# A two-layer encoder on one core: each step's rounded weights begin at an offset in their buffers

## The chip, the cores and the metric

The kernel runs on one core of one Trainium2 chip. The metric is the time of one execution on the device in microseconds. Before the change the median of two runs is 2566.06 us (2565.14 to 2566.98).

## What is computed

Two layers act on 256 tokens of width 2048. Each layer has three blocks, each with a residual sum: a mixer (projections `w_in` to three recurrences, then `w_out`), a cross attention to 256 memory rows, and a gated feed-forward block of width 5632. In short:

```python
for l in range(DEPTH):
    x = x + hybrid_mixer(rmsnorm(x, norm_mix[l]), ..., w_in[l], w_out[l], ...)
    x = x + memory_cross_attention(rmsnorm(x, norm_xattn[l]), rmsnorm(mem, norm_mem[l]), xa_wq[l], xa_wkv[l], xa_wo[l])
    x = x + conv_glu_ffn(rmsnorm(x, norm_ffn[l]), ffn_w_up[l], ffn_conv_w[l], ffn_conv_b[l], ffn_w_down[l])
return rmsnorm(x, norm_final)
```

All data are float32. Nearly all the work is `h @ w` with some 115 million weights in all, each of them read once from memory outside the core.

## The kernel before

The weights are cut into steps, in the order in which they are used (`layer_plan`, lines 64 to 119). A step holds seven or eight tiles of 128 x 128 weights (1024 or 896 columns in a buffer; two kinds are wider or take four row blocks at once). There are 890 steps. Each step's weights come by one DMA from the SyncE queue into a `raw` buffer (five of them).

A product of two float32 numbers is made of products of rounded ones (type float32r, which TensorE multiplies in one pass). So each weight is split into a rounded part `wh` and a rest `wl`: `split_w_hi` (line 1323) has ScalarE (ACT) copy `raw` to `wh` with rounding, and `split_w_lo` (line 1331) has VectorE (DVE) subtract `wh` from `raw` into `wl`. There are five `wh` and four `wl` buffers of WMAX = 1088 columns, that is 4352 bytes in each partition. The activations are split in the same way into a tile of 512 columns, rounded parts of 256 tokens and then the rests (`H`, and in later blocks `mo`, `mh`, `oT` and `g`).

The main loop (line 1450) goes through the steps: it issues the ACT split for the step three ahead, the DVE split for the step two ahead, and then this step's matmuls (`matmuls`, line 1345). A step of kind A takes each tile of weights as the stationary operand: with `form` 0, line 1360 multiplies the 512 moving columns with `wh`, and line 1361 the 256 rounded ones with `wl`. With `form` 1 (`xa_wo`, and the last tiles of all) there are three matmuls of 256 columns, lines 1363 to 1365. A step of kind B takes the activations as the stationary operand and the weights as the moving one, in slices of 256 or 264 columns (lines 1381 to 1383; 48 steps, 384 times three matmuls). Each matmul has a load of its stationary operand, which the profile shows apart as PEld.

Where things lie, in bytes in each partition: every `wh` and `wl` buffer begins at a place that is 64 modulo 256; a tile within it is 512 bytes further. `H`, and the pages that hold `mo`, `mh`, `oT` and `g`, begin at 224 modulo 256. Slices of 264 columns in kind B are 1056 bytes apart. Of the four slices of `UPAD` on which the convolutions work, two begin at an odd multiple of 16 bytes and two at a multiple of 32; the residual tiles `X` begin at a multiple of 32.

Between the steps' matmuls the loop runs the other work (norms, recurrences, attention, convolutions) as coroutines on ACT and DVE, with plain fp32 matmuls on TensorE. How many of them go ahead at each step is set by estimates of ACT's and DVE's time, which depend on the widths of the operands (`Metered`, lines 248 to 268).

Of the kernel before, what the change touches and what calls it, by code (L numbers as in the profile page):

```python
# [5 lines left out]
F32R = mybir.dt.float32r  # L6
# [5 lines left out]
P = 128  # L12
# [109 lines left out]
def step_len(st):  # L122
    if st["kind"] == "A":
        return P * len(st["tiles"])
    if st["kind"] == "B":
        return st["width"] * len(st["kts"])
    raise ValueError(st["kind"])
# [143 lines left out]
def build(tc, ws, xT, memT, par, con, masks, rot, dec, outT):  # L271
# [4 lines left out]
    pw = tc.alloc_tile_pool(name="weights", bufs=1)  # L276
# [39 lines left out]
    def nm(s):  # L316
        names[s] = names.get(s, 0) + 1
        return f"{s}_{names[s]}"
# [71 lines left out]
    def fn(out, src, f, **kw):  # L390

        want = "natural_log_exp_and_others" if f in (AF.Exp, AF.Ln) else "silu_and_others" if f in (AF.Silu, AF.Tanh) else table[0]
        if want != table[0]:
            act.preload_act_table_set(want)
            table[0] = want
        act.activation(out, src, f, **kw)

    def tt(out, a, b, op):
        dve.tensor_tensor(out, a, b, op)
# [900 lines left out]
    for l in range(NL):  # L1300
        gl, _ = group_steps(layer_plan(l))
        for off, g in gl:
# [3 lines left out]
            for st in g:  # L1306
                st = dict(st, l=l, g=gi, c=c, n=step_len(st))
# [4 lines left out]
    def load(gi):  # L1312
        if gi >= len(groups) or gi in raws:
            return
        l, off, g = groups[gi]
        t = pw.tile([P, GROUP_MAX], F32, name=nm("raw"), tag="raw", bufs=5)
        raws[gi] = t
        n = sum(step_len(st) for st in g)
        nc.sync.dma_start(t[:, :n], ws[l][off:off + P * n].rearrange("(p n) -> p n", p=P))

    WMAX = 1088

    def split_w_hi(j):
        if j < len(steps):
            st = steps[j]
            n = st["n"]
            st["raw"] = raws[st["g"]][:, st["c"]:st["c"] + n]
            st["wh"] = pw.tile([P, WMAX], F32R, name=nm("wh"), tag="wh", bufs=5)
            fn(st["wh"][:, :n], st["raw"], AF.Copy)

    def split_w_lo(j):
        if j < len(steps):
            st = steps[j]
            n = st["n"]
            st["wl"] = pw.tile([P, WMAX], F32R, name=nm("wl"), tag="wl", bufs=4)
            tt(st["wl"][:, :n], st["raw"], st["wh"][:, :n].bitcast(F32), ALU.subtract)
            if j + 1 == len(steps) or steps[j + 1]["g"] != st["g"]:
                load(st["g"] + 5)
            if j < 4:
                nc.sync.dma_start(X[2 + j // 2][:, j % 2 * 2:j % 2 * 2 + 2, :], xT[:, 8 + 2 * j:10 + 2 * j, :])  # L1340
# [46 lines left out]
    with tc.manual_schedule():  # L1387
# [57 lines left out]
        for j in range(2):  # L1445
            first_h(j)
            split_w_hi(j)
            split_w_lo(j)
        split_w_hi(2)
        for j, st in enumerate(steps):  # L1450
            if j == 0 or st["l"] != steps[j - 1]["l"]:
                for k, f in layer(st["l"]).items():
                    begins[(st["l"], k)] = f
            if 2 <= j + 2 < SINGLE + (KD - SINGLE) // 2:
                first_h(j + 2)
            split_w_hi(j + 3)
            split_w_lo(j + 2)
            for ev, ps in done:
                start(ev(ps), True)
            done.clear()  # L1460
            matmuls(st)
            if j == 5:
                fn(ONES, one, AF.Copy)
                nc.sync.dma_start(CON, con)
            if j == 7:
                nc.sync.dma_start(PAR[:, 0:PLAYER - KD], par[:, KD + T:PLAYER + T])
            if j == 11:
                nc.sync.dma_start(PAR[:, PLAYER - KD:], par[:, PLAYER + T:])
                mf = page(16, [P, 7, 64], F32, "mf")
                nc.sync.dma_start(mf, masks)  # L1470
                gp.tensor_copy(MSK, mf)
            if j == 15:
                start(gen_lb())
            advance(False)
            step_done(st["n"] / P * 0.325)
# [39 lines left out]
```

## Time and profile before

| | |
|---|---|
| median of two runs | 2566.06 us |
| the profiled execution | 2565.18 us, of which the span is 2563.3 us |
| TensorE busy | 2538.1 us (99%) |
| VectorE busy | 1925.6 us (75%) |
| ScalarE busy | 1469.8 us (57%) |
| mean granted share of TensorE's clock | 0.997 |

The span goes from the first to the last instruction. Matmuls overlap each other, so the pace of TensorE is read from the starts of matmuls, not from their durations.

### The profile page before, as it was taken

Reading aid. Unit: us, or ns where it says so; the run is one execution under the profiler, and the core shown is the slowest. Engines: PE = TensorE matmul, PEld = TensorE weight load, DVE = VectorE, ACT = ScalarE, POOL = GpSimd, SP = SyncE. Lnnn points to the kernel's source line nnn. Section 1 sums busy time; section 2 is a strip of 40 time slices with the busy share of each in tenths; the row PEclk is TensorE's granted clock in tenths of the full one; section 3 lists DMA queues with packets and bytes.
Section 4 is the critical chain, followed back from the end, with each engine's and each line's share of the span. In section 5 each row is a group of like instructions: output and inputs, shape, how many; then the busy total and the mean of one; then the engine's idle time right before and its main releaser. Section 6 shows DMA issues by size and latency. Waiting matters only on the chain.

```text
span 2563.3 us, 40208 instructions
## 1 busy us (share of the span) xinstructions
PE 2538.1 (99%) x15456; PEld 2252.9 (88%) x15456; DVE 1925.6 (75%) x3028; ACT 1469.8 (57%) x2152; POOL 4.9 (0%) x12
## 2 busy tenths in 40 slices
PE   9999989999999999999999999999999999999998
PEld 8888978998888888888898888889988888888887
DVE  7998788768776567776678888876877765677765
ACT  6866566566554345555466756655665543555543
POOL 0000000000000000000000000000000000000000
PEclk9999999999999999999999999999999999999999
DMA  7556656556665666665665575675566666666664
GB/s 272 170 170 205 194 161 197 186 172 190 190 190 183 193 195 192 190 189 186 191 192 163 154 236 181 189 217 170 175 196 189 189 187 191 194 188 193 189 183 131
DMA packets 141104, 482.02 MB, mean 188 GB/s; under 512 B 15280, under 2 KB 21360, under 8 KB 140912
## 3 DMA queue, kind: packets, MB, share of 16 engines
q1 hardware_dynamic: 140624, 479.17, 60.4%
q8 instruction: 122, 2.00, 0.3%
q14 instruction: 70, 0.57, 0.1%
q10 hardware_dynamic: 288, 0.27, 0.0%
HBM read 477.25 MB, written 2.13 MB: 187 GB/s over the span
## 4 chain that ended last, share of the span: by engine, by line
PE 97%; DVE 2%; DMA 0%; ACT 0%; issue 0%; DVEq 0%; SPq 0%; ACTq 0%
PE pj L1360 57%; PE pj L1361 29%; PE pj L1381 2%; PE pj L1382 2%; PE pj L1383 2%; PE pj L1364 1%; PE pj L1363 1%; PE pj L1365 1%; DVE wl L267 1%; PE ms L798 0%; PE ms L700 0%; PE ms L964 0%; DVE w L267 0%; DVE xbc L267 0%; PE ms L1152 0%; PE ms L1186 0%
## 5 line engine op out<-in xcount | busy, mean ns | idle before, releaser
L1360 PE MATMUL pj<-H,wh 128*128 128x512 f32 x4480 | 1561.0, 393 | 0.5 <-DVE H L267 0.5
L267 DVE TENSOR_TENSOR wl<-raw,wh 128x1024 fp32r<-128x1024 f32 (+2 forms) x894 | 1076.4, 1206 | 418.3 <-PE pj L1361 220.8
L267 ACT ACTIVATE wh<-raw 128x1024 fp32r<-128x1024 f32 (+2 forms) x894 | 933.4, 1048 | 658.2 <-PE pj L1360 351.8
L1361 PE MATMUL pj<-H,wl 128*128 128x256 f32 x4480 | 1253.1, 280 | 4.1 <-DVE wl L267 4.1
L1360 PEld LDWEIGHTS pj<-H,wh 128*128 128x128 f32 x4480 | 841.4, 188 | 186.5 <-ACT wh L267 1.1
L1361 PEld LDWEIGHTS pj<-H,wl 128*128 128x128 f32 x4480 | 841.5, 188 | 6.4 <-DVE wl L267 5.8
L1360 PE MATMUL pj<-g,wh 128*128 128x512 f32 x1386 | 480.7, 392 | 0.0
L1361 PE MATMUL pj<-g,wl 128*128 128x256 f32 x1386 | 387.4, 280 | 0.0
L1360 PEld LDWEIGHTS pj<-g,wh 128*128 128x128 f32 x1386 | 260.2, 188 | 57.4
L1361 PEld LDWEIGHTS pj<-g,wl 128*128 128x128 f32 x1386 | 260.2, 188 | 0.0
L267 ACT COPY e<-pj 128x256 f32<-128x256 f32 x288 | 106.4, 370 | 240.9 <-PE pj L1361 236.1
L1360 PE MATMUL pj<-mo,wh 128*128 128x512 f32 x512 | 179.7, 395 | 7.2 <-DVE mo L267 7.2
L267 DVE SCALAR_TENSOR_TENSOR ya<-UPAD,PAR,ya 128x256 f32<-128x256 f32 x352 | 146.5, 478 | 0.0
L1361 PE MATMUL pj<-mo,wl 128*128 128x256 f32 x512 | 143.9, 281 | 0.0
L267 DVE TENSOR_TENSOR X<-X,pj 128x256 f32<-128x256 f32 x167 | 70.0, 420 | 83.3 <-PE pj L1361 73.7
L1360 PEld LDWEIGHTS pj<-mo,wh 128*128 128x128 f32 x512 | 97.1, 190 | 29.2 <-DVE mo L267 7.6
L1361 PEld LDWEIGHTS pj<-mo,wl 128*128 128x128 f32 x512 | 97.1, 190 | 0.0
L267 ACT ACTIVATE ya<-UPAD,PAR 128x256 f32<-128x256 f32 x176 | 94.9, 588 | 1.2 <-DVE g L267 1.2
L267 DVE TENSOR_TENSOR UPAD<-pj,e 128x256 f32<-128x256 f32 x208 | 86.4, 418 | 0.2
L267 DVE TENSOR_TENSOR UPAD<-UPAD,R 128x512 f32<-128x512 f32 (+1 forms) x120 | 74.3, 621 | 4.0
L1381 PE MATMUL pj<-wh,H 128*128 128x264 f32 (+1 forms) x256 | 73.1, 285 | 0.0
L1383 PE MATMUL pj<-wh,H 128*128 128x264 f32 (+1 forms) x256 | 72.6, 284 | 0.0
(283 smaller groups left out, 1956.4 us busy)
## 6 DMA issues: line engine op xcount, KB each, us to landing
raw<-ws SPq DMA_DIRECT2D x778, 512.0 KB, 4.1
raw<-ws SPq DMA_DIRECT2D x96, 448.0 KB, 3.4
raw<-ws SPq DMA_DIRECT2D x16, 528.0 KB, 3.9
DE<-CD SPq DMA_DIRECT2D x8, 512.0 KB, 4.6
ya<-memT SPq DMA_DIRECT2D x16, 256.0 KB, 4.9
DS<-CD SPq DMA_DIRECT2D x8, 256.0 KB, 5.9
X<-xT SPq DMA_DIRECT2D x6, 256.0 KB, 7.2
outT<-y SPq DMA_DIRECT2D x3, 512.0 KB, 2.9
```

Of the source, the lines that this page charges most:

```text
L267: return f(out, *a, **k)
L1360: pe.matmul(ps, wh[:, a], s, start=first, stop=False)
L1361: pe.matmul(ps[:, :T], wl[:, a], s[:, :T], start=False, stop=last)
L1363: pe.matmul(ps[:, :T], wh[:, a], s[:, :T], start=first, stop=False)
L1364: pe.matmul(ps[:, :T], wh[:, a], s[:, T:], start=False, stop=False)
L1365: pe.matmul(ps[:, :T], wl[:, a], s[:, :T], start=False, stop=last)
L1381: pe.matmul(ps, xh, wh[:, a], start=f, stop=False)
L1382: pe.matmul(ps, xh, wl[:, a], start=False, stop=False)
L1383: pe.matmul(ps, xl, wh[:, a], start=False, stop=e)
```

## The change

The buffers get a first column `o` from which each step's `wh` and `wl` begin. In steps of kind A it is 4 x (j mod 16) columns, j being the number of the step: 0, 16, 32, ... 240 bytes, and then 0 again. In steps of kind B it is 16 columns, 64 bytes. The ACT and DVE splits and the matmuls all work on the shifted slices. The buffers' number, length and addresses stay, and the instructions of every engine, their order, their widths and what they wait for are the same.

```diff
--- before.py
+++ after.py
@@ -1325,14 +1325,16 @@
             st = steps[j]
             n = st["n"]
             st["raw"] = raws[st["g"]][:, st["c"]:st["c"] + n]
-            st["wh"] = pw.tile([P, WMAX], F32R, name=nm("wh"), tag="wh", bufs=5)
+
+            st["o"] = o = 16 if st["kind"] == "B" else 4 * (j % 16)
+            st["wh"] = pw.tile([P, WMAX], F32R, name=nm("wh"), tag="wh", bufs=5)[:, o:]
             fn(st["wh"][:, :n], st["raw"], AF.Copy)
 
     def split_w_lo(j):
         if j < len(steps):
             st = steps[j]
             n = st["n"]
-            st["wl"] = pw.tile([P, WMAX], F32R, name=nm("wl"), tag="wl", bufs=4)
+            st["wl"] = pw.tile([P, WMAX], F32R, name=nm("wl"), tag="wl", bufs=4)[:, st["o"]:]
             tt(st["wl"][:, :n], st["raw"], st["wh"][:, :n].bitcast(F32), ALU.subtract)
             if j + 1 == len(steps) or steps[j + 1]["g"] != st["g"]:
                 load(st["g"] + 5)
```

## Rows read from the trace of the kernel before

**Rows 1.** The page: span, busy time by engine, granted clock by slice, chain by engine.

```profile
span 2563.3 us, 40208 instructions
...
PE 2538.1 (99%) x15456; PEld 2252.9 (88%) x15456; DVE 1925.6 (75%) x3028; ACT 1469.8 (57%) x2152; POOL 4.9 (0%) x12
...
PEclk9999999999999999999999999999999999999999
...
PE 97%; DVE 2%; DMA 0%; ACT 0%; issue 0%; DVEq 0%; SPq 0%; ACTq 0%
```

**Rows 2.** Waits: engine, line, releaser: us in total, times, longest.

```profile
ACT wh L267 <- PE pj L1360: 351.8, 260, 4.7
...
DVE wl L267 <- PE pj L1361: 220.8, 212, 1.7
```

**Rows 3.** Groups of line 1360: shapes, count | busy us, mean ns | idle.

```profile
L1360 PE MATMUL pj<-H,wh 128*128 128x512 f32 x4480 | 1561.0, 393 | 0.5 <-DVE H L267 0.5
...
L1360 PE MATMUL pj<-g,wh 128*128 128x512 f32 x1386 | 480.7, 392 | 0.0
...
L1360 PE MATMUL pj<-mo,wh 128*128 128x512 f32 x512 | 179.7, 395 | 7.2 <-DVE mo L267 7.2
...
L1360 PE MATMUL pj<-mh,wh 128*128 128x512 f32 x128 | 45.0, 395 | 0.0
```

**Rows 4.** Timeline of PE, 800 to 804 us: start us, us, line, tiles.

```profile
799.68 0.39 PE L1360 MATMUL pj<-g,wh 128*128 128x512 f32 x1
799.91 0.28 PE L1361 MATMUL pj<-g,wl 128*128 128x256 f32 x1
...
803.84 0.39 PE L1360 MATMUL pj<-g,wh 128*128 128x512 f32 x1
```

**Rows 5.** Timeline of PE, eight fp32 matmuls in one row; their group.

```profile
529.87 1.89 PE L1186 MATMUL ms<-prT,v 128*128 128x256 f32 x8
...
L1186 PE MATMUL ms<-prT,v 128*128 128x256 f32 x32 | 7.6, 379 | 0.0
```

**Rows 6.** Timeline of PE in wo, first and last of 44 rows.

```profile
539.80 0.28 PE L1363 MATMUL pj<-oT,wh 128*128 128x256 f32 x1
...
544.91 0.28 PE L1364 MATMUL pj<-oT,wh 128*128 128x256 f32 x1
```

**Rows 7.** Timeline of PE in kind B of 256 columns, 42 rows.

```profile
503.76 0.28 PE L1382 MATMUL pj<-wl,mh 128*128 128x256 f32 x1
...
508.68 0.28 PE L1381 MATMUL pj<-wh,mh 128*128 128x256 f32 x1
```

**Rows 8.** Timeline of PE in kind B of 264 columns, 44 rows.

```profile
1339.75 0.29 PE L1382 MATMUL pj<-wl,H 128*128 128x264 f32 x1
...
1345.00 0.28 PE L1383 MATMUL pj<-wh,H 128*128 128x264 f32 x1
```

**Rows 9.** Timeline of PE at the end, 66 rows of 256 columns.

```profile
2542.10 0.28 PE L1363 MATMUL pj<-g,wh 128*128 128x256 f32 x1
...
2549.73 0.28 PE L1365 MATMUL pj<-g,wl 128*128 128x256 f32 x1
```

**Rows 10.** Timeline of PE, six intervals of 264 columns.

```profile
57.76 0.28 PE L1381 MATMUL pj<-wh,H 128*128 128x264 f32 x1
...
58.38 0.29 PE L1383 MATMUL pj<-wh,H 128*128 128x264 f32 x1
58.51 0.29 PE L1381 MATMUL pj<-wh,H 128*128 128x264 f32 x1
```

**Rows 11.** Groups of DVE by form: wl, UPAD and X.

```profile
L267 DVE TENSOR_TENSOR wl<-raw,wh 128x1024 fp32r<-128x1024 f32 x778 | 948.7, 1222 | 324.5 <-PE pj L1361 178.5 <-issue 117.3 <-PE pj L1382 7.7
...
L267 DVE TENSOR_TENSOR UPAD<-pj,e 128x256 f32<-128x256 f32 x208 | 86.4, 418 | 0.2
L267 DVE TENSOR_TENSOR X<-X,pj 128x256 f32<-128x256 f32 x167 | 70.0, 420 | 83.3 <-PE pj L1361 73.7 <-PE pj L1365 7.2
```

**Rows 12.** A stretch: us, busy us of each engine (instructions), PEclk, DMA.

```profile
533.00:552.00 19.00, 19.00 (x162) 19.00 (x161) 18.49 (x35) 13.16 (x22) 0.00 (x0) 1.00 0.64 194
```

## The prediction, made before the change was run

> **What bounds the kernel now.** I read the page's busy line first, then the chain, the waits, and last the starts of single matmuls in the timeline. The reader sees in [rows 1] that TensorE (PE) is busy 2538.1 of 2563.3 us and carries 97% of the chain that ended last, and that its granted clock is at the top digit in every slice, so it runs at 2.4 GHz of its two levels. The waits [rows 2] say the same from the other side: the two engines that split the weights, ScalarE (ACT) and VectorE (DVE), wait for PE to hand back buffers (351.8 us for `wh`, 220.8 us for `wl`); PE waits for neither over any length. So only what changes PE's own pace can change the time much.
>
> What is that pace? Nearly all of it is the pair of lines 1360 and 1361. The four groups of line 1360 [rows 3] count 4480 + 1386 + 512 + 128 = 6506 tiles, and each tile has one matmul of 512 columns with `wh` and one of 256 columns with `wl`, so 13,012 matmuls, each with a weight load of its own. The mean durations in those rows (392 to 395 ns) are of no use for pace, since matmuls overlap. Starts are: in [rows 4] the same matmul starts at 799.68 and, twelve tiles later, at 803.84, that is 4.16 / 12 = 346.7 ns a tile. At one column a cycle, 768 columns at 2.4 GHz are 320.0 ns. The excess is 26.7 ns a tile, 13.3 ns for each matmul with its load, and 13.3 x 13,012 = 173 us of the whole run. This excess is the only thing the change can act on.
>
> Where does it come from? [Rows 5] show plain fp32 matmuls with weight loads of the same 128 columns: eight starts lie within 1.89 us less the last one's 379 ns, so 1.51 / 7 = 216 ns for 256 columns. That is two cycles a column (213.3 ns) and an excess of only 2.4 ns. So loading weights is nearly free beside a stream that is read at half rate, and costs some 13 ns beside one that is read at full rate. That looks like two reads of on-chip memory that get in each other's way, the stream's and the load's, and then the addresses of the two may matter. How much they matter is the question of this case.
>
> **The change part by part.** No instruction is added, removed or moved, on any engine; widths and waits stay. What changes is where `wh` and `wl` begin. Before, each of their buffers is 4352 bytes (17 x 256) long, so all the weights of line 1360's tiles begin at the same place modulo 256, and the moving operands at another, 160 bytes on from it; both are multiples of 32 bytes. After, step j's weights lie 16 x (j mod 16) bytes further on. The steps of kind B, where the weights are the moving operand, get a fixed 64 bytes; that keeps their place modulo 64, and they are only 1152 matmuls, so I cost them at nothing; a nanosecond each would be 1 us.
>
> Of sixteen offsets, four (0, 64, 128, 192) keep the place modulo 64, eight keep it modulo 32, and eight land 16 past a multiple of 32, where PE reads nothing at full rate in this trace. So the price at most of the offsets is not shown and has to be bounded by the nearest rows, which are other full-rate stretches with other address pairs or widths:
> - `wo` tiles, three matmuls of 256 columns: 539.80 to 544.91 holds 43 intervals [rows 6], 118.8 ns each, excess 12.2 ns over 106.7.
> - kind B, 256 columns, weights moving: 503.76 to 508.68, 41 intervals [rows 7], 120.0 ns, excess 13.3.
> - kind B, 264 columns (110.0 ns), each slice 32 bytes further on in its place modulo 256: 1339.75 to 1345.00, 43 intervals [rows 8], 122.1 ns, excess 12.1.
> - The best stretch of all, 2542.10 to 2549.73, 65 intervals [rows 9]: 117.4 ns, excess 10.7.
> - The worst six in a row, 57.76 to 58.51, of 264 columns [rows 10]: 125.0 ns, excess 15.0. They follow a 264-column slice at another place that ran faster, so place does something, but only some nanoseconds.
>
> I therefore take: the four offsets that keep the place modulo 64 keep 13.3 ns. The other twelve get the mean of the first three stretches, (12.2 + 13.3 + 12.1) / 3 = 12.5 ns, because those are the nearest rows and the two ends lie about evenly around it. That is 0.8 ns less on three quarters of 13,012 matmuls: 0.8 x 9759 = 7.8 us less. The lower end puts all 13,012 at 10.7 ns: 2.6 x 13,012 = 34 us less. The upper end puts all at 15.0: 1.7 x 13,012 = 22 us more.
>
> The splits. ACT and DVE now write `wh` and `wl`, and DVE reads `wh`, from places 16 bytes apart. I cost that at nothing: DVE already writes UPAD, half of whose slices begin at an odd multiple of 16 bytes, and takes 418 ns on the mean for 256 columns there against 420 ns for X, which lies at multiples of 32 [rows 11]. What hides a small loss is the wait of [rows 2]; where the cover is gone is a stretch such as 533 to 552 us, where DVE is busy 18.49 of 19.00 us [rows 12]. It holds about eight splits of 1.22 us; were they 10% slower, the stretch would grow by 1 us, and the few stretches of this kind by less than 5 us together.
>
> The Trainium skill ("TensorE: Matmul & The Clock Gate", "Step-by-step: what each phase is for") says that PE has two independent read ports, so that loading the next weights takes nothing from the running matmul; the same page's "Back-to-back issue gap" gives N / 2.4 + 2.5 ns. By these a tile would take 215.8 + 109.2 = 325 ns, and no offset of the weights could matter, which is the second rival below. The trace's 346.7 ns in [rows 4] does not agree, and the measurement decides: something is lost beside a full-rate stream, and the 2.4 ns excess of [rows 5] is the only place where the rule holds.
>
> Sum: the profiled execution took 2565.18 us, a span of 2563.3 and 1.9 around it; 2565.18 - 7.8 = 2557.4. That run lies 0.9 us under the median of 2566.06, so I give 2558.
>
> **The rivals.**
> 1. Slower: a start 16 past a multiple of 32 bytes makes a load read more pieces, and it gets in the stream's way more often. The place is the eight odd offsets, 6506 matmuls; if their excess doubles, 13.3 x 6506 = 87 us, so 2653. It decides 2% (51.3 us) from 7.9 ns a matmul on, an excess of 21.2 ns. For it: nothing before reads at such a place, and single intervals of 264 columns reach 0.13 us in [rows 10]. Against it: over any stretch, excesses lie between 10.7 and 15.0.
> 2. Nothing: the excess is the price of a load beside a full-rate stream, whatever the addresses, and the change does not do what it could: 2566. For it: [rows 4] and [rows 7] have the same 13.3 ns with operands exchanged. Against it: the spread of [rows 8 to 10], and 12.2 ns in [rows 6] with the address pair of [rows 4].
> 3. Faster by over 2%: the loss is a meeting of the two reads at one place, and half of the offsets avoid it and fall to the 2.4 ns of [rows 5]: 10.9 x 6506 = 71 us, so 2495. For it: [rows 5] show that 2.4 ns is possible. Against it: no full-rate stretch goes below 10.7.
> 4. The splits become slower by more than their cover: some 5 us if small, over 2% only if DVE's 1.22 us grew by tens of per cent. [Rows 11] speak against it.
>
> **How the numbers follow.** Forecast (a small gain or loss between the two ends of the measured excesses) 0.50; nothing 0.32; slower at odd offsets 0.10; faster 0.06; splits 0.02. About 2% is what a measurement of this kernel can tell from no change. Faster by over 2%: 0.06 and 0.01 of the forecast's far end, 0.07. Slower: 0.10 and 0.01 of the splits, 0.11. Within 2%: 0.82. The range begins under the lower end (2566 - 34 = 2532) at 2528. Above it takes in the upper end (2566 + 22 = 2588) and that part of the first rival in which odd offsets lose 5.2 ns more (34 us): 2600.
>
> **What would show it.** Right: in the changed profile tiles of a step at offset 64 keep 346.7 ns, those at other offsets stand a nanosecond or two beside it, a different value for different steps but the same within a step; DVE's `wl` stays at 1222 ns, PE at 99%. Wrong: tiles at odd offsets that take over 360 ns (rival 1) or under 335 (rival 3); every step at 346.7 (rival 2); `wl` over 1300 ns and PE waiting for it (rival 4).

## The result, and the profile after the change

The changed kernel takes 2584.69 us (median of two runs, 2584.53 to 2584.85), before it was 2566.06 us: a ratio of 1.0072, with a 95% interval of 1.005 to 1.0093. It is 0.7% slower. The profiled execution took 2584.53 us, with a span of 2582.7.

The page of the changed kernel, the lines that answer to [rows 1]:

```profile
span 2582.7 us, 40208 instructions
...
PE 2557.2 (99%) x15456; PEld 2258.3 (87%) x15456; DVE 1925.8 (75%) x3028; ACT 1470.4 (57%) x2152; POOL 4.9 (0%) x12
...
PEclk9999999999999999999999999999999999999999
...
PE 98%; DVE 1%; DMA 0%; ACT 0%; issue 0%; DVEq 0%; SPq 0%; ACTq 0%
```

PE's busy time grew by 19.1 us (2538.1 to 2557.2) and the span by 19.4. PE is still the chain, now with 98%, and its clock is at the top digit throughout. The waits that answer to [rows 2] (engine, line, releaser: us in total, times, longest; the diff adds two lines, so 1360 is now 1362):

```profile
ACT wh L267 <- PE pj L1362: 362.8, 265, 4.8
...
DVE wl L267 <- PE pj L1363: 231.6, 225, 1.7
```

The splits wait a little longer for PE than before (362.8 against 351.8 us, 231.6 against 220.8), so they are not what became slower. DVE's split says it too: the group that answers to the first of [rows 11] (shapes, count | busy us, mean ns | idle before, releasers) still has 1222 ns. (Its groups of four widths count 778 + 96 + 16 + 4 = 894 steps, and this, not 890, is their number.)

```profile
L267 DVE TENSOR_TENSOR wl<-raw,wh 128x1024 fp32r<-128x1024 f32 x778 | 949.1, 1222 | 336.9 <-PE pj L1363 187.0 <-issue 122.4 <-PE pj L1384 7.6
```

The groups of line 1362 answer to [rows 3]. The counts are the same, and each mean is 2 ns longer:

```profile
L1362 PE MATMUL pj<-H,wh 128*128 128x512 f32 x4480 | 1574.7, 395 | 0.8 <-DVE H L267 0.8
...
L1362 PE MATMUL pj<-g,wh 128*128 128x512 f32 x1386 | 485.4, 394 | 0.0
...
L1362 PE MATMUL pj<-mo,wh 128*128 128x512 f32 x512 | 181.4, 397 | 7.2 <-DVE mo L267 7.2
...
L1362 PE MATMUL pj<-mh,wh 128*128 128x512 f32 x128 | 45.3, 397 | 0.0
```

These means are durations. The pace is in the starts, as in [rows 4]. Here are the starts of line 1362 in two steps of the changed kernel, one at offset 176 and one at offset 224 (start us, us, line, tiles):

```profile
848.08 0.39 PE L1362 MATMUL pj<-g,wh 128*128 128x512 f32 x1
...
850.51 0.39 PE L1362 MATMUL pj<-g,wh 128*128 128x512 f32 x1
...
897.39 0.40 PE L1362 MATMUL pj<-g,wh 128*128 128x512 f32 x1
...
899.16 0.40 PE L1362 MATMUL pj<-g,wh 128*128 128x512 f32 x1
```

At offset 176 seven tiles take 850.51 - 848.08 = 2.43 us, 347 ns each, as before. At 224, after the first tile, five take 1.77 us, 354 ns each; rounding leaves up to 2 ns open in either. So the steps differ. When all starts within a step are sorted by offset, leaving out tiles over 375 ns, every offset has a mean of its own, from 347.0 ns (160) to 353.3 ns (16), and none lies under the 346.7 of before; the table below has them. The mean over offsets is 349.7 ns, and 3.0 x 6506 = 19.5 us. Kind B's matmuls of 256 columns went the other way, from 119.9 to 118.1 ns on the mean over all their starts, 1.8 x 768 = 1.4 us less.

The means leave out one loss. At offset 64, and at no other, 43 of the 50 steps of kind A have one tile of 388 ns, nearly always the first one after the move from offset 48:

```profile
155.56 0.42 PE L1362 MATMUL pj<-H,wh 128*128 128x512 f32 x1
...
155.95 0.39 PE L1362 MATMUL pj<-H,wh 128*128 128x512 f32 x1
```

The kernel before has none. At some 38 ns over the other tiles of this offset they come to 1.6 us. The sum is then 19.5 - 1.4 + 1.6 = 19.7 us, against the span's 19.4.

### The profile page after: what moved, and what is told of

It is laid out like the page before. It is cut to its first block, busy times and chain, and to the rows that moved or that the text cites. A ratio compares the mean times of both kernels' runs of the same rounds, so it can differ in the third digit from the quotient of the medians.

```text
span 2582.7 us, 40208 instructions
## 1 busy us (share of the span) xinstructions
PE 2557.2 (99%) x15456; PEld 2258.3 (87%) x15456; DVE 1925.8 (75%) x3028; ACT 1470.4 (57%) x2152; POOL 4.9 (0%) x12
## 4 chain that ended last, share of the span: by engine, by line
PE 98%; DVE 1%; DMA 0%; ACT 0%; issue 0%; DVEq 0%; SPq 0%; ACTq 0%
PE pj L1362 58%; PE pj L1363 30%; PE pj L1383 2%; PE pj L1385 2%; PE pj L1384 2%; PE pj L1366 1%; PE pj L1367 1%; PE pj L1365 1%; PE ms L798 0%; PE ms L700 0%; DVE wl L267 0%; PE ms L964 0%; PE ms L1152 0%; PE ms L1186 0%; DMA raw<-ws 0%; DVE w L267 0%
## 5 line engine op out<-in xcount | busy, mean ns | idle before, releaser
L267 DVE TENSOR_TENSOR wl<-raw,wh 128x1024 fp32r<-128x1024 f32 (+2 forms) x894 | 1076.8, 1207 | 433.6 <-PE pj L1363 231.6
L267 ACT ACTIVATE wh<-raw 128x1024 fp32r<-128x1024 f32 (+2 forms) x894 | 934.0, 1048 | 672.6 <-PE pj L1362 362.8
```

What stands on the lines that cost most here:

```text
L267: return f(out, *a, **k)
```

## The experiments

All of them start from the kernel before; each one's diff shows the offset (in columns of 4 bytes) that `wh` gets, and `wl` where it differs. Every kernel computes the whole of the reference. Two theories stood at the start: that each place of the weights has its own pace ("the place"), and that pace is lost whenever the weights move from one step to the next ("the move").

**1. Kind A alone.**

```diff
+            st["o"] = o = 0 if st["kind"] == "B" else 4 * (j % 16)
```

> Only the steps of kind A get the cycle of sixteen; kind B stays at 0. Both theories: the whole loss of the change lies in kind A, whose 6506 tiles went from 346.7 to 349.7 ns in the changed kernel's trace (3.0 x 6506 = 19.4 us), while kind B's 768 matmuls of 256 columns became 1.8 ns faster (1.4 us). So 2566 + 19 + 1.5, about 2586 us. Were the 64 bytes of kind B the cause, it would be 2566.

Measured: 2586.62 us, ratio 1.0081 (1.0066 to 1.0097). As expected, the loss is all in kind A.

**2. Kind B alone.**

```diff
+            st["o"] = o = 16 if st["kind"] == "B" else 0
```

> Only the steps of kind B get 64 bytes; kind A stays at 0. Both theories: kind A's tiles at 346.7 ns as before, kind B's matmuls of 256 columns at 118.1 ns as in the changed kernel instead of 119.9, so 1.8 x 768 = 1.4 us less, 2564.7 us, too little to tell from the kernel before by time; the trace decides. If the gain of kind B came from what stood before it (the offsets of kind A), its pace is 119.9.

Measured: 2564.28 us, ratio 0.9995 (0.9986 to 1.0004): not to be told from before by time. The timeline of a stretch of kind B with 256 columns, the first and the last of 85 rows:

```profile
263.82 0.28 PE L1382 MATMUL pj<-wh,H 128*128 128x256 f32 x1
...
273.67 0.28 PE L1382 MATMUL pj<-wh,H 128*128 128x256 f32 x1
```

That is 9.85 us for 84 intervals, 117.3 ns each, against 120.0 in [rows 7]; over all such starts it is 117.7 against 119.9. The gain of kind B is its own, it is real in the trace, and it is worth some 1.6 us.

**3. The offset moves on only after sixteen steps.**

```diff
+            st["o"] = o = 0 if st["kind"] == "B" else 4 * (j // 16 % 16)
```

> Kind A's offset moves on only after sixteen steps (16 x ((j div 16) mod 16) bytes), kind B at 0. Theory of the place (each place of the weights has its own pace): each offset shows within its block the pace that tiles 5 to 8 of a step showed in the changed kernel, between 346.5 and 353.3 ns, on the mean 349.4, so 2.75 x 6506 = 18 us more, 2584 us. Theory of the move (the pace is lost in the first tiles after the weights have moved): all blocks settle at 346.7, there are about 55 moves instead of 842, so at most 2 us more, 2568 us. Both at work: between, near 2576.

Measured: 2585.42 us, ratio 1.0076 (1.0062 to 1.0089). The theory of the place had 2584, that of the move 2568. Starts of line 1361 (line 1360 of before) in a block at offset 208 and in one at 224:

```profile
659.90 0.39 PE L1361 MATMUL pj<-H,wh 128*128 128x512 f32 x1
...
664.06 0.39 PE L1361 MATMUL pj<-H,wh 128*128 128x512 f32 x1
...
709.92 0.40 PE L1361 MATMUL pj<-H,wh 128*128 128x512 f32 x1
...
714.16 0.40 PE L1361 MATMUL pj<-H,wh 128*128 128x512 f32 x1
```

Each pair of rows spans twelve tiles: 4.16 / 12 = 346.7 ns at 208 and 4.24 / 12 = 353.3 ns at 224. The means over all starts of a tile, in ns, worked out from the two traces:

| offset, bytes | 0 | 16 | 32 | 48 | 64 | 80 | 96 | 112 |
|---|---|---|---|---|---|---|---|---|
| changed kernel | 348.3 | 353.3 | 350.7 | 349.2 | 350.4 | 351.5 | 349.8 | 348.5 |
| blocks of sixteen steps | 346.8 | 353.3 | 350.9 | 349.4 | 350.2 | 350.1 | 349.9 | 349.8 |

| offset, bytes | 128 | 144 | 160 | 176 | 192 | 208 | 224 | 240 |
|---|---|---|---|---|---|---|---|---|
| changed kernel | 348.1 | 351.7 | 347.0 | 348.4 | 348.1 | 347.7 | 352.2 | 350.2 |
| blocks of sixteen steps | 346.7 | 352.3 | 347.1 | 346.7 | 351.0 | 346.7 | 353.2 | 353.1 |

With a fifteenth of the moves the mean over the offsets is 349.8, with all of them 349.7. The moves cost little: after one, the first tiles can lie over the place's own pace (at offset 0 they begin with 352 ns and end with 346.7) or under it (at 224 they begin with 345 and go on with 353.3). What they do cost is the 1.6 us of the tiles of 388 ns; run 1, with every move, took 1.2 us longer than this run. One entry of the table hides something: offset 192 has 353.2 ns in two of its three blocks and 346.7 in the third, so its 351.0 is a mean of two paces.

**4 and 6. One place for the whole run: 16 bytes, and 208 bytes.**

```diff
+            st["o"] = o = 0 if st["kind"] == "B" else 4
```

> All steps of kind A at 16 bytes, kind B at 0: no moves at all, and a place at which the changed kernel was slow (353.0 ns on the mean). Theory of the place: 353.3 ns in all tiles, 6.6 x 6506 = 43 us more, 2609 us. Theory of the move: 346.7 ns, 2566 us.

Measured: 2609.0 us, ratio 1.0169 (1.0155 to 1.0183), the very number of the theory of the place; no step of kind A moves in this kernel. Twelve tiles at the time of [rows 4]:

```profile
799.61 0.39 PE L1361 MATMUL pj<-H,wh 128*128 128x512 f32 x1
...
803.85 0.39 PE L1361 MATMUL pj<-H,wh 128*128 128x512 f32 x1
```

4.24 / 12 = 353.3 ns. The other run has 52 columns in place of 4:

> All steps of kind A at 208 bytes, kind B at 0. Theory of the place: 346.7 ns in all tiles, as in the blocks of 208 in the run before, so 2566 us, although 208 is an odd multiple of 16. Theory that an odd multiple of 16 bytes is slow in itself, which the run at 16 bytes left open: 353.3 ns, 2609 us.

Measured: 2567.07 us, ratio 1.0002 (0.9992 to 1.0012), and 4.16 / 12 = 346.7 ns:

```profile
799.66 0.39 PE L1361 MATMUL pj<-g,wh 128*128 128x512 f32 x1
...
803.82 0.39 PE L1361 MATMUL pj<-g,wh 128*128 128x512 f32 x1
```

So an odd multiple of 16 bytes is not slow in itself. The theory of the move has fallen, and so has my first rival.

**5 and 8. The moving operand is shifted instead.**

```diff
-    pa.tile([P, 40], F32, name="PAD")
+    pa.tile([P, 36], F32, name="PAD")
```

> All weights as before; the padding tile is 16 bytes shorter, so the pages that hold g, mo and mh (the moving operands of 2026 tiles) begin 16 bytes earlier, while H (4480 tiles) stays. Seen from these pages the weights lie 16 bytes later, as at offset 16. Theory that the distance between weights and moving operand decides: 353.3 ns in the tiles with g, mo and mh and 346.7 in those with H, so 6.6 x 2026 = 13 us more, 2579 us. Theory that the weights' own place decides: 346.7 ns in all, 2566 us.

Measured: 2566.93 us in one run, but this shows nothing: a tile of 144 bytes takes as much room as one of 160, so the pages had not moved, and this was the kernel before once more. The second attempt has 48 in place of 40 and does move them, by 32 bytes:

> All weights as before; the padding tile is 32 bytes longer, so the pages that hold g, mo and mh (the moving operands of 2026 tiles) begin 32 bytes later, while H (4480 tiles) stays. Seen from these pages the weights lie 32 bytes earlier, as at offset 224. Theory that the distance between weights and moving operand decides: 353.2 ns in the tiles with g, mo and mh and 346.7 in those with H, so 6.5 x 2026 = 13 us more, 2579 us. Theory that the weights' own place decides: 346.7 ns in all, 2566 us.

Measured: 2576.85 us, ratio 1.0041 (1.0026 to 1.0056). Starts of line 1361 in tiles with `H`, and then in tiles with `g`:

```profile
699.56 0.39 PE L1361 MATMUL pj<-H,wh 128*128 128x512 f32 x1
...
703.72 0.39 PE L1361 MATMUL pj<-H,wh 128*128 128x512 f32 x1
...
819.86 0.40 PE L1361 MATMUL pj<-g,wh 128*128 128x512 f32 x1
...
824.10 0.40 PE L1361 MATMUL pj<-g,wh 128*128 128x512 f32 x1
```

4.16 / 12 = 346.7 ns with `H`, 4.24 / 12 = 353.3 ns with `g`, though the weights lie where they lay before. So the place of the moving operand counts too, and 32 bytes more for it give what 32 bytes less for the weights gave in run 3 (offset 224). As paces near 353 are common, this match alone could be chance. Form 1, which reads `oT` from the moved pages, has a rarer one. In the changed kernel its starts lie 113.6 ns apart at offset 224, and between 116.8 and 120.4 at the nine other offsets that occur there; in run 8 the same step, at offset 0, has the pace of 224. The first and last of 24 starts, in the changed kernel and then in run 8:

```profile
544.08 0.28 PE L1365 MATMUL pj<-oT,wh 128*128 128x256 f32 x1
...
546.69 0.28 PE L1367 MATMUL pj<-oT,wl 128*128 128x256 f32 x1
...
545.60 0.28 PE L1364 MATMUL pj<-oT,wh 128*128 128x256 f32 x1
...
548.21 0.28 PE L1366 MATMUL pj<-oT,wl 128*128 128x256 f32 x1
```

Both are 2.61 / 23 = 113.5 ns; the kernel before has 118.7 in this step. It is the distance between the weights and the moving operand that decides, as far as one distance, reached from either side and in two forms, can show it. (The time went up by 10 us beside the kernel before on the same chip, 3 less than foreseen. Some 2 of them were won elsewhere: over all starts, form 1 went from 118.3 to 114.4 ns, and the third of kind B that has `mh` as its stationary operand from 119.9 to 117.8.)

**7. The two kinds of weights apart.**

```diff
+            st["o"] = o = 16 if st["kind"] == "B" else 4 * (j // 3 % 16)
...
+            ol = 16 if st["kind"] == "B" else 4 * (j // 48 % 16)
```

> The two kinds of weights are moved apart: wh moves on by 16 bytes after every 3 steps, wl after every 48, so that nearly all 256 pairs of places occur for three steps each; kind B at 64. If the pace is set by each load alone (the load of wl falls beside the matmul of 512 columns, that of wh beside the one of 256), the two intervals depend each on its own place, and pairs such as wh at 160 (115.0 ns) with wl at 128 (228.6 ns) make tiles of 343.6 ns, under the 346.7 of before. If the two loads only work together (the sum of a tile snaps to a few values, 346.7 and 353.3), no pair falls under 346.7. The time is a mean over good and bad pairs: about 2585 us by either.

Measured: 2582.16 us in one run, against some 2585. The starts, without the first four tiles after a move, give a mean for 242 of the 256 pairs. 87 of them lie at 346.0 to 347.5 ns, 98 between that and 352.5, 49 above; four lie between 342 and 346, and four under: `wh` at 224 with `wl` at 48 or 176 (340.2 ns each), and `wh` at 96 with `wl` at 160 or 176 (341.6 and 341.7). The interval after a load does not follow that load's place alone: with `wh` at 160 and `wl` at 128, the pair that I had put together from the best halves, a tile has 353.0. So the two loads work together, yet there are pairs under 346.7, which neither of the two expectations had right.

**9. One of the best pairs for the whole run.**

```diff
+            st["o"] = o = 16 if st["kind"] == "B" else 56
...
+            ol = 16 if st["kind"] == "B" else 12
```

> Every step of kind A has wh at 224 and wl at 48 bytes, kind B at 64: the pair that had 340.2 ns a tile in three steps of the scan. Theory that a pair of places has a pace of its own that holds over the whole run: 340.2 ns in all 6506 tiles, 6.5 x 6506 = 42 us less, and 1.4 us from kind B, 2522 us. If the low pace came from what stood before those three steps, the tiles go back to 346.7 or 353.3 ns and the time lies between 2564 and 2609 us.

Measured: 2537.04 us, ratio 0.9886 (0.9869 to 0.9902), between the two expectations. Starts of line 1362 early in the run and in the feed-forward block:

```profile
19.75 0.40 PE L1362 MATMUL pj<-H,wh 128*128 128x512 f32 x1
...
23.95 0.40 PE L1362 MATMUL pj<-H,wh 128*128 128x512 f32 x1
...
799.65 0.39 PE L1362 MATMUL pj<-g,wh 128*128 128x512 f32 x1
...
803.74 0.39 PE L1362 MATMUL pj<-g,wh 128*128 128x512 f32 x1
```

4.20 / 12 = 350 ns at 20 us, and 4.09 / 12 = 341 ns (over all starts of such stretches 340.0) at 800 us. The same pair has two lasting paces. A fifth of the tiles have 349 to 351 ns, and 0.2 x 6506 x 10 ns = 13 us is most of the 15 us that the time misses to 2522.

**10. The pair's neighbourhood in steps of 4 bytes.**

```diff
+            st["o"] = o = 16 if st["kind"] == "B" else 52 + j // 12 % 9
...
+            ol = 16 if st["kind"] == "B" else 8 + j // 108 % 8
```

> The pair's neighbourhood in steps of 4 bytes: wh at 208, 212, ... 240 bytes, moving on after every 12 steps, wl at 32, 36, ... 60 bytes, moving on after every 108; kind B at 64. If the places matter in units of 16 bytes, the pairs show four by four the same pace; if the pace depends on the place in units of 4 bytes, each has its own, and some may lie under 340. The time is a mean: about 2570 us by either.

Measured: 2586.37 us in one run, 16 more than I had given. Pairs do not go four by four: with `wh` at 224, the means for `wl` at 32, 36, ... 60 are 350.3, 341.1, 351.6, 346.7, 342.2, 346.7, 346.7 and 340.1 ns. So places count in units under 16 bytes, as far as a stretch of twelve steps for each pair can tell, since run 9 has shown that a pair can have two paces. No pair lies under 340.0.

**11 and 12. Two pairs that kept 340 ns in that run.** In the first, `wl` begins at column 15, with the rest as in 9; in the second `wh` begins at 59 and `wl` at 9.

> As the run before with wh at 224, but wl at 60 bytes, a pair that kept 340.1 ns through its twelve steps in the fine scan. Theory that each pair has one pace: 340 ns throughout, 2522 us. Theory that a pair has several stable paces and the stretch before chooses: stretches at 349 to 351 ns again, which in the run before made up a fifth of the tiles, so about 2537 us, more or less as the pair is caught more or less often.

Measured: 2524.45 us, ratio 0.984 (0.9824 to 0.9857). The page, and the starts at the same two times as in 9:

```profile
span 2521.9 us, 40208 instructions
...
PE 2495.2 (99%) x15456; PEld 2225.2 (88%) x15456; DVE 1924.7 (76%) x3028; ACT 1469.0 (58%) x2152; POOL 4.9 (0%) x12
```

```profile
19.65 0.39 PE L1362 MATMUL pj<-H,wh 128*128 128x512 f32 x1
...
24.07 0.39 PE L1362 MATMUL pj<-H,wh 128*128 128x512 f32 x1
...
799.55 0.39 PE L1362 MATMUL pj<-g,wh 128*128 128x512 f32 x1
...
803.97 0.39 PE L1362 MATMUL pj<-g,wh 128*128 128x512 f32 x1
```

4.42 / 13 = 340.0 ns at both times. With `wl` 12 bytes further on than in run 9, hardly any tile has the other pace; these 12 bytes lie within one unit of 16, so over whole runs too a unit of 16 bytes is too coarse. This version beats both kernels: 41 us under the one before in its own comparison.

> The same with wh at 236 and wl at 36 bytes, a pair that had 340.0 ns in all its tiles in the fine scan. One pace for each pair: 2522 us. Several stable paces: stretches of 347 to 353 ns beside those of 340, and a time between 2522 and 2566 us.

Measured: 2636.64 us, ratio 1.0275 (1.026 to 1.0291), slower than I had allowed for. Its starts:

```profile
19.81 0.39 PE L1362 MATMUL pj<-H,wh 128*128 128x512 f32 x1
...
23.89 0.39 PE L1362 MATMUL pj<-H,wh 128*128 128x512 f32 x1
...
799.73 0.40 PE L1362 MATMUL pj<-H,wh 128*128 128x512 f32 x1
...
804.04 0.40 PE L1362 MATMUL pj<-H,wh 128*128 128x512 f32 x1
```

4.08 / 12 = 340.0 ns at 20 us, as in the fine scan, and 4.31 / 12 = 359 ns at 800 us; nine tenths of its tiles have 360 ns. One pair of places, the same matmuls, and two paces that both last.

## Why the prediction was wrong, point by point

- **The direction was wrong.** I forecast 8 us less and it was 19 us more. The measured time lies within my range, and within 2%, as I had held likeliest, but on the other side of no change. My sign of being right fails too: tiles at offset 64 were to keep 346.7 ns, and have 350.4 with one of 388 in most steps.
- **The bound and the place were right.** PE's pace was what changed, and nearly all of it in the tiles of line 1360. ACT and DVE were not slowed by starts at multiples of 16 bytes: their splits of 1024 columns keep 1061 and 1222 ns on the mean. The excess of [rows 4] does depend on addresses. Runs 4, 6 and 8 show it.
- **The step that failed is the price at the other places**: "The other twelve get the mean of the first three stretches". Those stretches [rows 6 to 8] have another form, 256 or 264 columns at every load, and form decides as well as place: at offset 224 the pair of 512 and 256 columns is among its slowest (353.2 ns), and three matmuls of 256 are at their fastest (113.6). So their excess said nothing on the pair of 512 and 256. At those twelve offsets run 3 has 350.2 ns a tile on the mean, an excess of (350.2 - 320) / 2 = 15.1 ns a matmul, where I took 12.5; the changed kernel has 15.0, which makes some 16 of the 19.5 us. That this is nearly the upper of my two bounds is luck, as the bound came from [rows 10], another form.
- **The step before it failed too:** "the four offsets that keep the place modulo 64 keep 13.3 ns". In run 3 offsets 0 and 128 do; 64 has 350.2 ns, and 192 has 346.7 in one block and 353.2 in two. In the changed kernel the four have an excess of 14.4 ns a matmul on the mean, the other 3 us. There is no sign of a rule in multiples of 64, nor of 16.
- **The price of kind B at nothing** was right in size: 1.6 us less in run 2.
- **Rival 1** (odd multiples of 16 are slow) is refuted by offsets 176 and 208, which have 346.7 ns. **Rival 2** (the address does not matter) is refuted by run 4. **Rival 3** named a lower pace that the change did not reach: none of the sixteen common offsets of `wh` and `wl` has a mean under 346.7 ns, but run 11 has 340.0 with two offsets, an excess of 10 ns a matmul, still far from the 2.4 of [rows 5].
- I had read the kernel's own place as one draw among many, with an excess above the mean of its neighbours. It was among the best of the sixteen. Only the same form at other places could have told so, and the trace of before has no second place for it. So the direction was not to be had there, and the forecast should have been no change, with both ends open.

The Trainium skill ("TensorE: Matmul & The Clock Gate", "Step-by-step: what each phase is for") says that loading the next weights takes nothing from the running matmul, as PE has two independent read ports. The runs do not agree: by that rule the tiles of run 4, those with `g` in run 8 and those of run 12 would have the pace of before, and they have 353.3, 353.3 and, nine tenths of the last, 360 ns.

What stays open: why a distance gives the pace it does, which of two lasting paces a pair falls into, and why the move from 48 to 64 bytes costs a tile of 388 ns. The runs show that these exist; none shows the mechanism.

## What to carry to other kernels

Where TensorE is the bound and reads its moving operand at full rate, the place of the stationary operand relative to the moving one is worth a scan: here it moved the whole kernel between 2524 and 2637 us with no instruction added or removed. Don't spread the operands over places, since a mean over places is worse than a good one; hold one place, choose it by the starts of matmuls in a trace rather than by a rule of alignment, give the two kinds of weights places of their own, and time the choice over the whole run, because a place can have two paces.

## What was not expected of the hardware

- The steadiest paces of a tile are 340.0, 346.7, 353.3 and 360.0 ns, that is 6.67 ns apart, 16 cycles at 2.4 GHz. Others last too: 350.0 ns at offset 64 in run 3 (single tiles have 349 to 351), and 353 at 240, where tiles of some 345 and 361 ns alternate.
- A pace once taken can last for hundreds of tiles. In runs 9 and 12 it changes only after other matmuls or a pause of PE; run 12 had 340 and 360 ns at the same addresses.
- Places count in units under 16 bytes: with `wh` at 224, `wl` at 48 leaves a fifth of the tiles at 350 ns over a whole run, at 60 nearly none. In run 10 even 4 bytes make a difference (346.7 ns at 56, 340.1 at 60), in one stretch of twelve steps each.
